# An encoder layer on one core: the first quarter of the MLP in a fixed block order, the residual's four VectorE transposes moved into the first block

## The chip, the core and the metric

The kernel runs on one core of a Trainium2 chip. A core has a matrix engine (TensorE, PE in the profile, with PEld for the loading of its stationary operand), a vector engine (VectorE, DVE), an activation engine (ScalarE, ACT), a general engine (GpSimd, POOL) and SyncE (SP), which here issues almost all transfers between the chip's memory and the core's buffers. Each engine works through its own list of instructions in order; the lists meet only in semaphores. The metric is the device time of one execution in microseconds (us), as the median of several runs.

## The reference

One layer of a streaming encoder for 256 tokens of width 2048, all in float32: a mixer (retention and a gated delta rule side by side), cross-attention into 256 memory tokens, and an MLP with squared ReLU, each with a norm ahead of it and a residual behind it. The change touches the passage from cross-attention into the MLP:

```python
    x = x + cross_attention(h, mem_n, w_xq[l], w_xkv[l], w_xo[l])
    h = rms_norm(x, norm_ffn_g[l])
    x = x + jnp.square(jax.nn.relu(h @ w_ff1[l])) @ w_ff2[l]
return rms_norm(x, norm_final_g)
```

`w_ff1` is 2048 x 8192, `w_ff2` 8192 x 2048.

## The kernel before

**Products.** Every float32 matrix is split into a rounded part and its remainder (`hi` and `lo`, both float32r), and a product is the sum of three partial products. Weights come in pieces of 1 MB: `fetch` (line 104) issues one transfer into a `raw` buffer of 128 x 2048, and for each half of it one ScalarE instruction that rounds (L125, `whi` from `raw`) and one VectorE instruction that subtracts (L126, `wlo` from `raw` and `whi`), each over 128 x 1024. There are three `raw` buffers and three of `whi` and of `wlo`. From the MLP on there is a fourth pair, `whx` and `wlx`, which `half_tiles` (line 79) hands out for every fourth half. Its pool (`mlp`, line 1117) takes the memory that the cross-attention's pool held until then.

**Blocks.** `blocks_in_steps` (line 192) computes 256 output columns for all tokens: two pieces of weights, so four halves, and for each half one *step* of 16 matmuls (L210; 8 of 128 x 512 on `whi`, 8 of 128 x 256 on `wlo`), spread over two accumulators `s0` and `s1`. Behind the last step each accumulator is read out (L219 on ScalarE, L220 on VectorE) and handed to an `evac` function. In the MLP that is `evac_h`: squared ReLU, and the split of the result into `hid`. The function takes a list `ends`. If it isn't empty, each matmul is issued after the last one that stands in it, and each step adds its last matmul to it: the steps are then held in the order of the code.

**What sets the order.** The kernel is written against a scheduler that orders each engine's list when the program is built, by priorities and by its own estimate of when things are ready. `tc.high_priority` lets a fetch overtake; `tc.issue_after(x)` puts an instruction behind `x`. What the scheduler chose is fixed in the program.

**The MLP.** It runs in four quarters of 2048 hidden columns (`fb`, line 1374): eight blocks with `w_ff1`, then products with `w_ff2`. Quarters 1 to 3 pass `ends` to their blocks; the first quarter passes `None`, so its steps may be interleaved. Below, A is the first block of the first quarter and B the second, with steps A0 to A3 and B0 to B3. The halves of A3 and B3 are `whx` and `wlx`.

**The residual.** `rt` holds the residual with features on the partitions. The output is wanted with tokens on the partitions, in `res`. Ahead of the first quarter four VectorE instructions (lines 1121 and 1122, STREAM_TRANSPOSE of 128 x 1024) transpose 32 x 32 squares of `rt` into `tr`, and `place` (line 1124), called behind each of the eight blocks, issues four transfers of 64 KB that put the squares in their places (L1129, `res` from `tr`, in runs of 128 bytes). A `place` needs all four transposes. `rt` and `tr` are later used as weight buffers.

**The norm.** Behind the last block of cross-attention's output projection, two small matmuls (L1042) add up the squares `acc2`; then come L1044 on VectorE, a power on POOL (L266) and L1113 on VectorE. Only the additions into `res`, much later, need their result.

Of the kernel before, what the change touches and what calls it, by code (L numbers as in the profile page):

```python
# [18 lines left out]
D = 2048  # L19
# [33 lines left out]
def trunk(ctx: ExitStack, tc: tile.TileContext, x_f, mem_f, positions, lead_f, small_f, w_in, ret_gn_g, w_out, w_xq,  # L53
# [3 lines left out]
    act, vec, pool, pe = nc.scalar, nc.vector, nc.gpsimd, nc.tensor  # L57
# [9 lines left out]
    def stream_ps():  # L67
        s0 = psp.tile([P, 512], F32, name="s0", tag="s0", bufs=2)
        s1 = psp.tile([P, 512], F32, name="s1", tag="s1", bufs=2)
        return s0, s1  # L70

    def bank():
        return psp.tile([P, 512], F32, name="b", tag="b", bufs=4)


    fetched, steps, latest = [], [], {}
# [18 lines left out]
    def step():  # L95
        if steps and next(steps[0], steps) is steps:
            steps.pop(0)
# [6 lines left out]
    def fetch(pieces, k, n, cuts=1, hold=None, at=(0, 0)):  # L104

        raw = wp.tile([P, k * n], F32, name="raw", tag="raw", bufs=3)
        rv = raw.rearrange("p (k n) -> p k n", k=k)
        with tc.high_priority(offset=100000):
            for off, ap in pieces:
                src = ap.rearrange("(k p) n -> p k n", p=P)  # L110
                for c in range(cuts):
                    ks = slice(c * k // cuts, (c + 1) * k // cuts)
                    fetched.append(nc.sync.dma_start(rv[:, ks, off:off + ap.shape[1]], src[:, ks, :]).ins)
            got = []
            for i in range(2):
                if hold:
                    both = hold().both
                    hi, lo = (both[:, a:a + 2, :].rearrange("p a s -> p (a s)") for a in (0, 2))
                else:
                    hi, lo = (h[:, a:a + k * n // 2] for h, a in zip(half_tiles(), at))  # L120
                src = raw[:, i * k * n // 2:(i + 1) * k * n // 2]
                part = k * n // max(cuts, 2)
                for c in range(0, k * n // 2, part):
                    cs = slice(c, c + part)
                    latest["hi"] = act.activation(hi[:, cs], src[:, cs], AF.Copy).ins  # L125
                    latest["lo"] = vec.tensor_sub(lo[:, cs], src[:, cs], hi[:, cs].bitcast(F32)).ins  # L126
                got.append((hi.rearrange("p (k n) -> p k n", n=n), lo.rearrange("p (k n) -> p k n", n=n)))
            latest["raw"] = fetched[-1]
        return got
# [20 lines left out]
    def quad_a():  # L150
        return new_quad(hqp, 5)
# [40 lines left out]
    def blocks_in_steps(quads, w, c0, nb, evac, ends=None, even=False):  # L192

        k = 16 // nb
        ps = stream_ps()
        n = nb * P
        for g in range(KT // k):  # L200
            halves = fetch([(0, w[g * k * P:(g + 1) * k * P, c0:c0 + n])], k, n, at=AT_BLOCKS)
            for h in range(2):
                these = [(i, b, part) for i in range(k // 2) for b in range(nb) for part in range(2)]
                if even and g == h == 0:
                    these.sort(key=lambda a: a[2])
                for i, b, part in these:
                    kk = (2 * g + h) * k // 2 + i
                    x = quads[kk // 4][0] if part else quads[kk // 4].both
                    with tc.issue_after(ends[-1]) if ends else ExitStack():
                        ins = pe.matmul(ps[b][:, :S] if part else ps[b], halves[h][part][:, i, b * P:(b + 1) * P],  # L210
                                        x[:, kk % 4, :], start=kk == 0 and not part, stop=kk == KT - 1 and part == 1).ins
                if ends is not None:
                    ends.append(ins)
                step()
                yield
        for b in range(nb):
            with tc.high_priority(offset=50000):
                o = sm.tile([P, S], F32, name="bo", tag="bo", bufs=2)
                act.activation(o, ps[b][:, S:], AF.Copy)  # L219
                vec.tensor_add(o, o, ps[b][:, :S])  # L220
                evac(b, o)

    def blocks(*args, **more):
        for _ in blocks_in_steps(*args, **more):
            pass
# [26 lines left out]
    with tc.high_priority(offset=300000):  # L252
# [3 lines left out]
        early = bank()  # L256
# [738 lines left out]
    rt = tp.tile([P, KT, S], F32, name="rt", tag="rt", bufs=1)  # L995
# [115 lines left out]
    h3, rstd3 = residual_pass(att, w_xo[0], G_FFN, "n3", between=values)  # L1111
# [6 lines left out]
    res = fp.tile([P, NT, D], F32, name="res", tag="res", bufs=1)  # L1118

    tr = fp.tile([P, KT, S], F32, name="tr", tag="tr", bufs=1)  # L1120
    for c in range(4):
        vec.transpose(*(a[:, 4 * c:4 * c + 4, :].rearrange("p k s -> p (k s)") for a in (tr, rt)))

    def place(b8):

        with tc.issue_after(fetched[-1]):
            for a in range(4):
                to = res[b8 % 4 * 32:b8 % 4 * 32 + 32, b8 // 4, :].rearrange("i (k a f) -> i k a f", a=4, f=32)[:, :, a, :]
                nc.sync.dma_start(to, tr[32 * a:32 * a + 32, :, b8 * 32:b8 * 32 + 32])  # L1129
# [44 lines left out]
    def token_sums(i, hs):  # L1174

        sv = fp.tile([P, 4, P], F32, name="sv", tag="sv", bufs=1)
        (a11, a21), (a12, a22) = ((hs[:, b, 0:P], hs[:, b, P:S]) for b in range(2))
        vec.tensor_add(sv[:, 0], a21, a22)
        vec.tensor_sub(sv[:, 1], sv[:, 0], a11)
        vec.tensor_sub(sv[:, 2], a11, a21)  # L1180
        vec.tensor_sub(sv[:, 3], a12, sv[:, 1])
        split([a[:, i, :] for a in s_hl], sv.rearrange("p a s -> p (a s)"))
# [190 lines left out]
    ends = []  # L1373
    for fb in range(4):
        hid = []
        rows = w_ff2[0, fb * D:(fb + 1) * D, :]
        early = fb > 0
        parts_of = with_seven(hid, rows, fb == 3, early)
        ends.clear()
        for b2 in range(8):  # L1380
            hs = fp.tile([P, 2, S], F32, name="hs", tag="hs", bufs=2)
            if b2 % 2 == 0:
                hid.append(quad_a())

            def evac_h(b, ps):
                if early:
                    act.activation(ps, ps, AF.Relu)
                    act.activation(hs[:, b, :], ps, AF.Square)
                else:
                    vec.scalar_tensor_tensor(hs[:, b, :], ps, 0.0, ps, op0=ALU.max, op1=ALU.mult)  # L1390
                qh, ql = (a[:, b2 % 2 * 2 + b, :] for a in hid[-1])
                act.activation(qh, hs[:, b, :], AF.Copy)
                vec.tensor_sub(ql, hs[:, b, :], qh.bitcast(F32))
                if b2 < 4 and b:
                    token_sums(b2, hs)

            blocks(h3, w_ff1[0], fb * D + b2 * 256, 2, evac_h, ends if early else None)
            if early and b2 > 2:
                next(parts_of)
            if fb == 0:  # L1400
                place(b2)
        for _ in parts_of:
            pass
# [42 lines left out]
```

## Time and profile before

| | |
|---|---|
| median of 3 runs | 2045.87 us (2045.28 to 2046.57) |
| the profiled execution: its own time | 2046.63 us |
| the profiled execution: span from first to last instruction | 2045.0 us |
| granted TensorE clock, mean over the span | 0.999 |
| 1 MB pieces of `w_ff1` and `w_ff2` into `raw` | 100 |
| transposes L1122 | 1360.0 to 1364.6 us of the span |
| place transfers L1129 | 1364.7 to 1421.9 us of the span |

The profile's page gives for each engine its busy time and share of the span, a chain of waits that is followed back from the last instruction, and groups of instructions by source line. The trace behind it answers finer questions: the timeline (instructions in order of time, with what ended the idle time ahead of each in square brackets), sums by stretches of time, and totals of who waited for whom. A matmul's shown duration is a latency: in a dense stream the next one starts before it ends, so that paces are read from starts. Lines of a queue (SPq) show the issue of transfers, not the transfers.

### The profile page before, as it was taken

The numbers are of one execution on the slowest core, as the hardware profiler recorded it, in microseconds if no ns is written. First come the engines' busy times: TensorE is split into PE (matmuls) and PEld (weight loads), VectorE is DVE, ScalarE is ACT, GpSimd is POOL, SyncE is SP. The second block draws the span as 40 slices with busy tenths as digits, with TensorE's granted clock in tenths as the row PEclk, the third lists the DMA queues.
The fourth block names the chain that finished last, engine by engine and source line by source line (L and its number), as shares of the span: only waits on it lengthen the run. The fifth ranks groups of instructions, "written<-read, shape, count | busy, mean of one in ns | idle before, by whom it ended". The sixth has DMA issues, their size and how long they took to land.

```text
span 2045.0 us, 28450 instructions
## 1 busy us (share of the span) xinstructions
PE 2032.4 (99%) x10802; PEld 1752.2 (86%) x10802; DVE 1548.7 (76%) x2422; ACT 1184.9 (58%) x1941; POOL 38.6 (2%) x50
## 2 busy tenths in 40 slices
PE   9999999999999999999999999999999999999998
PEld 8888888988888888888888899888888888888886
DVE  5887788779667875788567666777867887888788
ACT  6665764575457554755446565555546656656655
POOL 0000000000000000000000000000000000000000
PEclk9999999999999999999999999999999999999999
DMA  9679556456555655555467655569657656655761
GB/s 330 208 256 305 187 186 198 150 183 206 180 166 184 199 189 165 189 181 187 158 212 243 191 185 164 170 179 259 216 168 233 219 164 213 201 204 166 240 232 62
DMA packets 329225, 405.24 MB, mean 198 GB/s; under 512 B 34928, under 2 KB 239360, under 8 KB 328960
## 3 DMA queue, kind: packets, MB, share of 16 engines
q1 hardware_dynamic: 328656, 402.74, 61.3%
q8 instruction: 84, 1.38, 0.3%
q10 hardware_dynamic: 432, 0.69, 0.1%
q14 instruction: 53, 0.43, 0.1%
HBM read 389.74 MB, written 11.55 MB: 196 GB/s over the span
## 4 chain that ended last, share of the span: by engine, by line
PE 95%; DVE 2%; DMA 2%; ACT 1%; issue 0%; SPq 0%; POOLq 0%; POOL 0%; ACTq 0%; DVEq 0%
PE s L210 50%; PE s L167 8%; PE s L168 8%; PE s L166 8%; PE s L1212 7%; PE b L1212 7%; DMA raw<-w_ff 1%; PE s L400 1%; PE s L401 1%; PE s L402 1%; PE b L795 1%; PE b L698 1%; PE b L828 1%; PE b L138 0%; PE b L137 0%; PE b L139 0%
## 5 line engine op out<-in xcount | busy, mean ns | idle before, releaser
L210 PE MATMUL s<-q,whi 128*128 128x512 f32 x2816 | 968.7, 391 | 0.8 <-DVE bo L220 0.6
L126 DVE TENSOR_TENSOR wlo<-raw,whi 128x1024 fp32r<-128x1024 f32 x584 | 712.4, 1221 | 295.5 <-ACT whi L125 290.7
L125 ACT ACTIVATE whi<-raw 128x1024 fp32r<-128x1024 f32 x584 | 618.6, 1060 | 491.3 <-PE s L210 207.0
L210 PE MATMUL s<-q,wlo 128*128 128x256 f32 x2816 | 764.5, 281 | 0.4 <-DVE wlo L126 0.4
L210 PEld LDWEIGHTS s<-q,whi 128*128 128x128 f32 x2816 | 520.5, 188 | 101.7 <-DVE bo L220 0.9
L210 PEld LDWEIGHTS s<-q,wlo 128*128 128x128 f32 x2816 | 527.1, 188 | 13.2 <-DVE wlo L126 1.1
L167 PE MATMUL s<-wlo,q 128*128 128x512 f32 x704 | 277.3, 394 | 0.4 <-DVE wlo L126 0.4
L168 PE MATMUL s<-whi,q 128*128 128x512 f32 x704 | 274.9, 391 | 0.0
L166 PE MATMUL s<-whi,q 128*128 128x512 f32 x704 | 254.4, 391 | 0.0
L166 PEld LDWEIGHTS s<-whi,q 128*128 128x128 f32 x704 | 132.0, 188 | 27.3
L167 PEld LDWEIGHTS s<-wlo,q 128*128 128x128 f32 x704 | 132.3, 188 | 26.9 <-DVE wlo L126 0.8
L168 PEld LDWEIGHTS s<-whi,q 128*128 128x128 f32 x704 | 132.3, 188 | 26.3
L219 ACT ACTIVATE bo<-s 128x256 f32<-128x256 f32 x192 | 73.0, 380 | 108.5 <-PE s L210 108.4
L220 DVE TENSOR_TENSOR bo<-bo,s 128x256 f32<-128x256 f32 x192 | 79.7, 415 | 46.6 <-ACT bo L219 46.3
L1234 DVE TENSOR_TENSOR wlo<-rt,whi 128x1024 fp32r<-128x1024 f32 x56 | 68.1, 1223 | 32.8 <-ACT whi L1233 32.1
L125 ACT ACTIVATE whx<-raw 128x1024 fp32r<-128x1024 f32 x60 | 63.6, 1060 | 46.5 <-PE s L1212 19.1
L210 PE MATMUL s<-q,whx 128*128 128x512 f32 x256 | 89.2, 389 | 0.0
L1212 PE MATMUL s<-whi,q 128*128 128x512 f32 (+1 forms) x280 | 88.8, 383 | 0.0
L126 DVE TENSOR_TENSOR wlx<-raw,whx 128x1024 fp32r<-128x1024 f32 x60 | 73.3, 1221 | 19.2 <-ACT whx L125 18.8
L1233 ACT ACTIVATE whi<-rt 128x1024 fp32r<-128x1024 f32 x56 | 59.3, 1060 | 39.6 <-PE s L1212 20.2
L1212 PE MATMUL b<-whi,q 128*128 128x512 f32 x220 | 71.5, 389 | 0.0
L210 PE MATMUL s<-q,wlx 128*128 128x256 f32 x256 | 70.4, 280 | 0.0
(344 smaller groups left out, 2373.0 us busy)
## 6 DMA issues: line engine op xcount, KB each, us to landing
raw<-w_in SPq DMA_DIRECT2D x143, 1024.0 KB
raw<-w_ff SPq DMA_DIRECT2D x100, 1024.0 KB
raw<-w_xkv SPq DMA_DIRECT2D x29, 1024.0 KB
raw<-w_out SPq DMA_DIRECT2D x16, 1024.0 KB
raw<-w_xq SPq DMA_DIRECT2D x16, 1024.0 KB
raw<-w_xo SPq DMA_DIRECT2D x16, 1024.0 KB
rt<-w_ff SPq DMA_DIRECT2D x14, 1024.0 KB
tr<-w_ff SPq DMA_DIRECT2D x14, 1024.0 KB
```

What stands on the lines that cost most here:

```text
L125: latest["hi"] = act.activation(hi[:, cs], src[:, cs], AF.Copy).ins
L126: latest["lo"] = vec.tensor_sub(lo[:, cs], src[:, cs], hi[:, cs].bitcast(F32)).ins
L166: pe.matmul(o, xh, wh, start=first, stop=False)
L167: pe.matmul(o, xh, wl, start=False, stop=False)
L168: pe.matmul(o, xl, wh, start=False, stop=last)
L210: ins = pe.matmul(ps[b][:, :S] if part else ps[b], halves[h][part][:, i, b * P:(b + 1) * P], x[:, kk % 4, :], start=kk == 0 and not part, ...
L219: act.activation(o, ps[b][:, S:], AF.Copy)
L220: vec.tensor_add(o, o, ps[b][:, :S])
L400: pe.matmul(o, xh, wh, start=kk == 0 and c0 == 0, stop=False)
L1212: ins = pe.matmul(o, lhs[l], rhs[r], start=key not in opened, stop=last and j == 2, skip_group_check=True).ins
L1233: latest["hi"] = act.activation(hi, raw[:, c:c + 1024], AF.Copy).ins
L1234: latest["lo"] = vec.tensor_sub(lo, raw[:, c:c + 1024], hi.bitcast(F32)).ins
```

## The change

The four transposes are taken out of the place ahead of the MLP. The first block of the first quarter is run step by step, and behind each of its four steps one transpose is emitted, to be issued after the latest weight subtraction (`latest["lo"]`) at that point. All blocks of the first quarter now pass `ends`, so that each step's matmuls are issued after the previous step's last one. The number of instructions stays as it is.

```diff
-    for c in range(4):
-        vec.transpose(*(a[:, 4 * c:4 * c + 4, :].rearrange("p k s -> p (k s)") for a in (tr, rt)))
+    def transpose(c):
+        with tc.issue_after(latest["lo"]):
+            vec.transpose(*(a[:, 4 * c:4 * c + 4, :].rearrange("p k s -> p (k s)") for a in (tr, rt)))
...
-            blocks(h3, w_ff1[0], fb * D + b2 * 256, 2, evac_h, ends if early else None)
+            for n, _ in enumerate(blocks_in_steps(h3, w_ff1[0], fb * D + b2 * 256, 2, evac_h, ends)):
+                if fb == b2 == 0:
+                    transpose(n)
```

What the scheduler makes of it, at three places. Ahead of them, and on TensorE from the fourth block on, each engine's order is as it was; lines from 1122 on have one number more in the changed kernel.

TensorE behind step A2 (the first row is its last matmul). `s0_13017` and `s1_13018` are A's accumulators and `s0_13127`, `s1_13128` B's; `whi_13131` is the half of B0. Before:

```order
L210 MATMUL s1_13018<-q_12575,wlo_13064 128x256
L210 MATMUL s0_13127<-q_12127,whi_13131 128x512
L210 MATMUL s0_13127<-q_12127,wlo_13132 128x256
L210 MATMUL s1_13128<-q_12127,whi_13131 128x512
L210 MATMUL s1_13128<-q_12127,wlo_13132 128x256
L210 MATMUL s0_13127<-q_12127,whi_13131 128x512
L210 MATMUL s0_13127<-q_12127,wlo_13132 128x256
L1042 MATMUL b_12993<-ones_75,acc2_12125 128x2 x2
L210 MATMUL s1_13128<-q_12127,whi_13131 128x512
```

Now (`s0_13013` and `s1_13014` are A's accumulators, `whx_13065` and `wlx_13066` the halves of A3):

```order
L210 MATMUL s1_13014<-q_12575,wlo_13062 128x256
L1042 MATMUL b_12993<-ones_75,acc2_12125 128x2 x2
L210 MATMUL s0_13013<-q_12784,whx_13065 128x512
L210 MATMUL s1_13014<-q_12784,whx_13065 128x512
L210 MATMUL s0_13013<-q_12784,wlx_13066 128x256
L210 MATMUL s1_13014<-q_12784,wlx_13066 128x256
L210 MATMUL s0_13013<-q_12784,whx_13065 128x512
L210 MATMUL s0_13013<-q_12784,wlx_13066 128x256
```

Before, B0, B1, the first two matmuls of A3, the last of B1 and B2 stood ahead of the other 14 of A3; now all of A3 stands directly behind A2 and the norm's two matmuls, and B0 behind A3.

VectorE at the transposes. `wlo_13174` is the lower half of B2, `wlx_13068` (before) and `wlx_13066` (now) that of A3. Before:

```order
L126 TENSOR_TENSOR wlo_13136<-raw_13129,whi_13135 128x1024
L126 TENSOR_TENSOR wlo_13174<-raw_13171,whi_13173 128x1024
L1044 TENSOR_SCALAR n3_s_12996<-b_12993 128x2
L1122 STREAM_TRANSPOSE tr_13007<-rt_10152 128x1024 x4
L126 TENSOR_TENSOR wlx_13068<-raw_13061,whx_13067 128x1024
L1113 TENSOR_TENSOR rstd3q_13000<-n3_r_12998 128x2
```

Now:

```order
L126 TENSOR_TENSOR wlo_13136<-raw_13129,whi_13135 128x1024
L1044 TENSOR_SCALAR n3_s_12996<-b_12993 128x2
L1123 STREAM_TRANSPOSE tr_13007<-rt_10152 128x1024 x2
L126 TENSOR_TENSOR wlo_13174<-raw_13171,whi_13173 128x1024
L1113 TENSOR_TENSOR rstd3q_13000<-n3_r_12998 128x2
L126 TENSOR_TENSOR wlx_13066<-raw_13059,whx_13065 128x1024
L1123 STREAM_TRANSPOSE tr_13007<-rt_10152 128x1024 x2
```

The four transposes have become two and two, with the lower halves of B2 and A3 between them. ScalarE's order is unchanged here: the rounding for B2 (`whi_13173`) stands ahead of the one for A3 (`whx`).

SyncE's queue from the sixth `w_ff1` piece on (`raw_13282` is the second piece of the third block, `raw_13350` and `raw_13392` those of the fourth, `raw_13461` and `raw_13503` those of the fifth). Before:

```order
L113 DMA raw_13240<-w_ff1 128x8x256
L1129 DMA res_13006<-tr_13007 32x16x32 x2
L113 DMA raw_13282<-w_ff1 128x8x256
L1129 DMA res_13006<-tr_13007 32x16x32 x3
L113 DMA raw_13350<-w_ff1 128x8x256
L1129 DMA res_13006<-tr_13007 32x16x32 x4
L113 DMA raw_13392<-w_ff1 128x8x256
L1129 DMA res_13006<-tr_13007 32x16x32 x7
L113 DMA raw_13461<-w_ff1 128x8x256
```

Now:

```order
L113 DMA raw_13240<-w_ff1 128x8x256
L113 DMA raw_13282<-w_ff1 128x8x256
L1130 DMA res_13006<-tr_13007 32x16x32 x8
L113 DMA raw_13350<-w_ff1 128x8x256
L1130 DMA res_13006<-tr_13007 32x16x32 x4
L113 DMA raw_13392<-w_ff1 128x8x256
L1130 DMA res_13006<-tr_13007 32x16x32 x4
L113 DMA raw_13461<-w_ff1 128x8x256
```

One piece has moved ahead of all place transfers, and eight of these stand together behind it; by `raw_13461` both orders have issued the same pieces and the same sixteen place transfers.

## The prediction, made before the changed kernel was run

> **What bounds the kernel now.** I read the page's busy times and its chain of waits first, then sums by stages around the change, then the timelines of the engines that meet there.
>
> ```profile
> PE 2032.4 (99%) x10802; PEld 1752.2 (86%) x10802; DVE 1548.7 (76%) x2422; ACT 1184.9 (58%) x1941; POOL 38.6 (2%) x50
> PE 95%; DVE 2%; DMA 2%; ACT 1%; issue 0%; SPq 0%; POOLq 0%; POOL 0%; ACTq 0%; DVEq 0%
> ```
>
> TensorE is busy for 2032.4 of 2045.0 us: the kernel ends when its matmuls are through. Only 12.6 us are left, and the stage table (length, then busy us of PE, PEld, DVE, ACT, POOL, granted clock, share of the DMA engines, GB/s) shows how few of them lie near the change:
>
> ```profile
> 1340.00:1357.60 17.60, 17.60 (x105) 15.58 (x104) 13.18 (x21) 9.55 (x16) 0.00 (x0) 1.00 0.56 172
> 1357.60:1370.40 12.80, 12.22 (x73) 10.54 (x72) 10.12 (x12) 5.49 (x7) 0.69 (x1) 1.00 0.57 140
> 1370.40:1390.00 19.60, 19.60 (x116) 17.32 (x115) 15.05 (x30) 10.16 (x18) 0.00 (x0) 1.00 0.96 197
> 1390.00:1396.00 6.00, 5.60 (x33) 4.74 (x32) 3.15 (x8) 2.32 (x3) 0.00 (x0) 1.00 1.09 315
> 1396.00:1440.00 44.00, 44.00 (x256) 38.79 (x255) 32.81 (x51) 23.82 (x36) 0.00 (x0) 1.00 1.05 296
> ```
>
> TensorE idles 0.58 us in the second stretch and 0.40 us in the fourth, nowhere else in 100 us. The timeline has both (start, duration, what, idle ahead of it):
>
> ```profile
> 1369.07 0.28 PE L210 MATMUL s<-q,wlx 128*128 128x256 f32 x1
> 1369.94 0.50 PE L210 MATMUL s<-q,whi 128*128 128x512 f32 x1 [0.58 <-DVE bo L220]
> ...
> 1394.89 0.39 PE L210 MATMUL s<-q,whi 128*128 128x512 f32 x1
> 1395.68 0.39 PE L210 MATMUL s<-q,wlo 128*128 128x256 f32 x1 [0.40 <-DVE wlo L126]
> ```
>
> By starts they cost more, since a matmul's tail otherwise lies under the next one. In the dense stream below a `whi` matmul takes 0.23 us to the next start and a `wlo` one 0.115 (1357.60 to 1357.94 for the pair). The first hole is 0.87 - 0.115 = 0.75, the second 0.79 - 0.23 = 0.56; the first matmul behind each has 0.11 more than its pace. Together 0.86 + 0.67 = 1.53 us: all that the change can win here.
>
> **The change, part by part.** The first row below is the first matmul behind A2; the next four stand around the norm's matmuls:
>
> ```profile
> 1357.60 0.39 PE L210 MATMUL s<-q,whi 128*128 128x512 f32 x1
> ...
> 1357.94 0.39 PE L210 MATMUL s<-q,whi 128*128 128x512 f32 x1
> ...
> 1358.51 0.28 PE L210 MATMUL s<-q,wlo 128*128 128x256 f32 x1
> 1358.63 0.50 PE L1042 MATMUL b<-ones,acc 128*128 128x2 f32 x4
> 1358.99 0.47 PE L210 MATMUL s<-q,whi 128*128 128x512 f32 x1
> ```
>
> Six matmuls of B0 stand ahead of L1042 (the order's rows), 3 pairs of 0.34, so A2 ends its stream at 1357.60. Everything ahead of that keeps its order, so I keep that time. Now the other two engines:
>
> ```profile
> 1354.83 0.42 DVE L1028 TENSOR_TENSOR acc<-acc,sq 128x256 f32<-128x256 f32 x1
> 1356.34 1.23 DVE L126 TENSOR_TENSOR wlo<-raw,whi 128x1024 fp32r<-128x1024 f32 x1 [1.09 <-ACT whi L125]
> 1358.82 1.23 DVE L126 TENSOR_TENSOR wlo<-raw,whi 128x1024 fp32r<-128x1024 f32 x1 [1.25 <-ACT whi L125]
> 1359.96 0.15 DVE L1044 TENSOR_SCALAR n_s<-b 128x2 f32<-128x2 f32 x1
> 1360.03 4.61 DVE L1122 STREAM_TRANSPOSE tr<-rt 128x1024 f32<-128x1024 f32 x4
> 1364.56 1.18 DVE L126 TENSOR_TENSOR wlx<-raw,whx 128x1024 fp32r<-128x1024 f32 x1
> 1365.67 0.15 DVE L1113 TENSOR_TENSOR rstd3q<-n_r 128x2 f32<-128x2 f32 x1
> 1365.74 1.22 DVE L126 TENSOR_TENSOR wlo<-raw,whi 128x1024 fp32r<-128x1024 f32 x1
> ...
> 1357.72 1.06 ACT L125 ACTIVATE whi<-raw 128x1024 fp32r<-128x1024 f32 x1 [1.42 <-PE s L210]
> 1359.17 1.06 ACT L125 ACTIVATE whx<-raw 128x1024 fp32r<-128x1024 f32 x1 [0.38 <-PE b L1042]
> 1363.86 2.01 ACT L125 ACTIVATE whi<-raw 128x1024 fp32r<-128x1024 f32 x2 [3.63 <-DMA raw<-w_ff]
> ```
>
> Before, the halves of A3 were late (`wlx` done only at 1365.74, behind all four transposes), but TensorE did not wait: B0, B1 and B2, 8.3 us of matmuls, stood ahead. **The order that is now held takes this cover away.** Step by step:
> - L1042 runs from 1357.60, as `acc` is ready since 1355.25, and gives its result 0.50 later, at 1358.10. The next matmul could start 0.36 behind its start (1358.63 to 1358.99), at 1357.96.
> - ScalarE still rounds B2's half first (from 1357.72, released by A2's last read), then `whx`, which waits for L1042 as before. Two in a row take 2.01: done at 1359.73. The two `whx` matmuls can start 0.05 later, 1359.78, and are out at 1360.35 (2 x 0.23 + 0.11).
> - VectorE: L1044 at 1358.14 and transposes from 1358.21. Four took 1360.03 to 1364.56, 1.13 each, so two end their turn at 1360.48. Then `wlo` for B2, 1.12 to the next start (as 1364.56 to 1365.67): 1361.60; L1113, 0.07 (POOL's power, 0.69 us by the stage table, is through by then); `wlx` from 1361.67, 1.18: 1362.85.
> - TensorE takes up the other 14 matmuls of A3 0.05 later, at 1362.90 (as in the second hole, where the subtraction of the row below ends at 1395.63 and the matmul starts at 1395.68). They take 2.29 + 0.11: A3 ends at 1365.30. Without waits it would end at 1357.96 + 8 x 0.344 = 1360.71.
>
> ```profile
> 1394.40 1.23 DVE L126 TENSOR_TENSOR wlo<-raw,whi 128x1024 fp32r<-128x1024 f32 x1 [2.85 <-ACT whi L125]
> ```
>
> The new stall is **4.59 us**. Were two transposes, two subtractions and both small operations not pipelined, it would be 0.41 longer (1.20 + 1.20 + 1.23 + 1.18 + 0.30 against 4.71, with L1122's single duration taken as a quarter of 4.61 + 3 x 0.07): 5.0. Were `whx` alone the limit, with `wlx` right behind it at 1360.9, it would be 2.6.
>
> **What is given back.** The first hole waited for A's read-out, as A was finished only shortly ahead of the third block. Now A ends a whole block earlier, at 1365.30, and the third block starts at about 1376.3: that wait goes, 0.86. The second hole waited for the fifth block's first piece:
>
> ```profile
> 1366.20 6.75 DMA raw<-w_ff
> 1376.75 8.03 DMA raw<-w_ff
> 1386.69 6.51 DMA raw<-w_ff
> 1393.31 1.06 ACT L125 ACTIVATE whi<-raw 128x1024 fp32r<-128x1024 f32 x1 [4.05 <-DMA raw<-w_ff]
> ...
> 1364.72 1.39 SPq L1129 DMA_DIRECT2D res<-tr  x2
> 1378.08 8.51 SPq L1129 DMA_DIRECT2D res<-tr  x7
> ```
>
> In the chain a piece takes 6.5 to 8.0 us from issue to landing. Every transfer behind the transposes is the question here, and SP's queue is where it is decided: `raw_13282` now waits for `wlx`'s read of its buffer (1362.85), then eight place transfers for the last transpose (1365.2, before 1364.7), and `raw_13350`, `raw_13392`, `raw_13461` stand behind those. Seven of them took 8.51 when the engines were full. Eight then end at about 1373 to 1375, `raw_13350` lands by 1383 and is needed at 1387.3 - 2.4 (one rounding, one subtraction). By `raw_13461` the queue has issued what it had before, from a start 0.5 later with one piece already out: it should be issued at 1386 to 1388 and land by 1394.5. TensorE wants it at 1394.89 - 0.86 + 4.59 = 1398.6, less 2.4. So the second hole closes too, 0.67, with 1.7 us to spare.
>
> **Sum**: + 4.59 - 0.86 - 0.67 = **+3.1 us**. No instruction is added, and behind the fifth block TensorE alone sets the pace to the end, so the shift stays. The span goes from 2045.0 to 2048.1, the profiled execution's own time from 2046.63 to 2049.7; that one lay 0.76 above the median of the runs, 2045.87. I predict **2048.9**.
>
> About 0.2%, 4.1 us, is what a measurement of this kernel can tell from no change. The forecast is a loss below that.
>
> **Rivals.**
> - *The clock falls in the stall* (slower). TensorE would run 2 matmuls in the 4.9 us between 1358.0 and 1362.9. That idling costs the clock shows at the end of the span, behind the last matmul:
>
> ```profile
> 2035.68 0.28 PE L1212 MATMUL s<-whi,q 128*128 128x256 f32 x1
> ...
> 2036.00:2041.00 5.00, 0.00 (x0) 0.00 (x0) 3.35 (x12) 4.21 (x8) 0.84 (x2) 1.00 0.63 234
> 2041.20:2045.00 3.80, 0.00 (x0) 0.00 (x0) 0.00 (x0) 0.00 (x0) 0.00 (x0) 0.50 0.61 224
> ```
>
>  Full clock held for 5.0 us of idling, half of it was granted 0.2 us later. My longest gap is 2.55 us, half of that, which speaks against it; for it, that two matmuls may not count as work. If the clock fell all the same and took as long to return as there to fall (an estimate; no row shows a return), 5.2 us at half pace cost 2.6: 3.1 + 2.6, 2051.5. It decides from the idle length at which the clock gives way, anywhere between the 0.58 us that left it at 1.00 and 5 us. Chance 0.12. [...]
> - *The eight place transfers hold up the weights* (slower). If they take 1.75 each (as slow as 6.98 for four, in the row below), `raw_13461` slips by some 4 us to 1398.5 and TensorE waits 2 us: 2051. For it: the DMA share of 0.96 to 1.09 there. Against: the sixteen transfers ahead of that piece are the same as before. Chance 0.12.
>
> ```profile
> 1387.93 6.98 SPq L1129 DMA_DIRECT2D res<-tr  x4
> ```
>
> - *The change doesn't stall TensorE as I think* (not slower): `wlx` comes with `whx`, if the transposes take next to nothing where ScalarE is the later one. 2.6 - 1.5 = 1.1: 2047.0. Against it stands VectorE's list, in order. Chance 0.07.
>
> **How the numbers follow.** The forecast has 0.69; its own range, from a stall of 4.2 to 5.0 with 0.86 to 1.53 given back and half a microsecond of the median's own scatter, is 2048.1 to 2050.1. The 80% range, 2047.3 to 2051.0, takes in most of the rivals. Slower by over 0.2% (above 2049.96): both slower rivals and a little of the forecast's upper end, 0.28. Faster by over 0.2% would need 4.1 us where 1.53 lie idle: 0.02. Within: 0.70.
>
> **What would show it.** In the changed profile: VectorE with two transposes, a subtraction and then `wlx`; TensorE idle behind L1042 in two pieces, about 1.7 and 2.5 us, the second ended by `wlx`; no idle at the third and the fifth block. A granted clock under 1.00 in the 10 us behind would show the first rival, an idle ended by a `whi` or `wlo` of the fourth or fifth block behind a late DMA the second. I am wrong if TensorE doesn't wait at A3.

## The result, and the profile after

| | before | after |
|---|---|---|
| median | 2045.99 us (2044.80 to 2046.90, 8 runs) | 2051.32 us (2050.21 to 2052.48, 8 runs) |
| the profiled execution: its own time, span | 2046.63, 2045.0 | 2051.23, 2049.6 |
| granted clock, mean over the span | 0.999 | 0.997 |

The change makes the kernel slower: ratio 1.0027, 95% interval 1.0017 to 1.0038. That is 5.3 us where 3.1 were forecast, and 0.3 us above the upper end of the range. It is the case of the first rival.

The page after: busy times, and the chain of waits by engine.

```profile
PE 2034.2 (99%) x10802; PEld 1754.7 (86%) x10802; DVE 1551.3 (76%) x2422; ACT 1185.3 (58%) x1941; POOL 38.6 (2%) x50
PE 96%; DVE 2%; DMA 0%; issue 0%; ACT 0%; SPq 0%; POOLq 0%; POOL 0%; DVEq 0%; ACTq 0%
```

The same 10802 matmuls keep TensorE busy 1.8 us longer. No work was added, so some of it ran more slowly. TensorE's waits between 1350 and 1450 us (waiting line, what it waits for, total us, times, longest) are only two:

```profile
PE s L210 <- DVE wlx L126: 2.2, 1, 2.2
PE s L210 <- ACT whx L125: 1.7, 1, 1.7
```

Both old holes, in front of the third and the fifth block, are gone. The timeline of TensorE shows the new ones and what follows:

```profile
1357.73 0.50 PE L1042 MATMUL b<-ones,acc 128*128 128x2 f32 x4
1359.91 0.93 PE L210 MATMUL s<-q,whx 128*128 128x512 f32 x2 [1.68 <-ACT whx L125]
1363.07 0.80 PE L210 MATMUL s<-q,wlx 128*128 128x256 f32 x2 [2.23 <-DVE wlx L126]
1363.67 0.63 PE L210 MATMUL s<-q,whx 128*128 128x512 f32 x1
...
1364.31 0.63 PE L210 MATMUL s<-q,whx 128*128 128x512 f32 x1
...
1366.87 0.51 PE L210 MATMUL s<-q,whx 128*128 128x512 f32 x1
...
1367.33 0.39 PE L210 MATMUL s<-q,whi 128*128 128x512 f32 x1
```

Up to 1363.07 this is the predicted stall: idle in two pieces, the second ended by `wlx`. Behind it a pair of matmuls takes 0.64 us (1363.67 to 1364.31) where the dense stream before took 0.344, until about 1367. The other two engines did what the prediction said, in the same order and nearly at the same times:

```profile
1358.35 2.36 DVE L1123 STREAM_TRANSPOSE tr<-rt 128x1024 f32<-128x1024 f32 x2
1360.63 1.18 DVE L126 TENSOR_TENSOR wlo<-raw,whi 128x1024 fp32r<-128x1024 f32 x1
1361.73 0.15 DVE L1113 TENSOR_TENSOR rstd3q<-n_r 128x2 f32<-128x2 f32 x1
1361.80 1.22 DVE L126 TENSOR_TENSOR wlx<-raw,whx 128x1024 fp32r<-128x1024 f32 x1
1362.93 2.37 DVE L1123 STREAM_TRANSPOSE tr<-rt 128x1024 f32<-128x1024 f32 x2
...
1358.82 1.04 ACT L125 ACTIVATE whx<-raw 128x1024 fp32r<-128x1024 f32 x1
```

The cause of the slow matmuls stands in the table by stretches (length, busy us of PE, PEld, DVE, ACT, POOL with their instructions, granted clock, share of the DMA engines, GB/s). It is cut at 1360.28 and 1367.10, where the clock changes, and every 3.41 us between and around them. That is half of the 6.83 us at half clock here, and all of the time at half clock in the runs with the transposes behind B and with A free (below). Two expectations call such a stretch a window.

```profile
1356.86:1360.28 3.42, 1.74 (x12) 1.46 (x11) 2.85 (x4) 2.00 (x2) 0.70 (x1) 1.00 0.34 82
1360.28:1363.69 3.41, 1.18 (x5) 0.62 (x4) 3.41 (x5) 0.00 (x0) 0.00 (x0) 0.50 0.69 225
1363.69:1367.10 3.41, 3.41 (x12) 2.93 (x12) 1.61 (x2) 0.00 (x0) 0.00 (x0) 0.50 0.74 212
1367.10:1370.52 3.42, 3.42 (x21) 3.03 (x21) 2.93 (x7) 1.94 (x4) 0.00 (x0) 1.00 0.93 187
```

The clock is halved at 1360.28, in the middle of the stall, and comes back at 1367.10. Only the first gap, 1.68 us, lies ahead of the fall; the second begins at 1360.84 (1359.91 + 0.93), when the clock is at half already. The matmuls recorded in a stretch of 3.41 us are 21 at full clock and 12 at half.

**Where the time went.** Without a wait, A3 would have ended 0.36 + 8 x 0.344 behind the start of L1042 at 1357.73: 1360.84. B0 starts at 1367.33, 6.49 us late. At full clock the 14 matmuls behind the first `wlx` pair's start would have ended 2.40 after 1363.07, at 1365.47. So the late data cost 4.63 and the clock 1.86. Less the two holes, 1.53, that is +4.96; the medians differ by 5.3 (3.5 to 7.8 by the interval), the two spans by 4.6.

### The profile page after: what moved, and what is told of

Read it like the earlier page. It is cut to its first block, busy times and chain, and to the rows that moved or that the text cites. A ratio compares the mean times of both kernels' runs of the same rounds, so it can differ in the third digit from the quotient of the medians.

```text
span 2049.6 us, 28451 instructions
## 1 busy us (share of the span) xinstructions
PE 2034.2 (99%) x10802; PEld 1754.7 (86%) x10802; DVE 1551.3 (76%) x2422; ACT 1185.3 (58%) x1941; POOL 38.6 (2%) x50
## 4 chain that ended last, share of the span: by engine, by line
PE 96%; DVE 2%; DMA 0%; issue 0%; ACT 0%; SPq 0%; POOLq 0%; POOL 0%; DVEq 0%; ACTq 0%
PE s L210 51%; PE s L167 8%; PE s L168 8%; PE s L166 8%; PE s L1213 7%; PE b L1213 7%; PE s L400 1%; PE s L401 1%; PE s L402 1%; PE b L795 1%; PE b L828 1%; PE b L138 0%; PE b L137 0%; PE b L698 0%; PE b L139 0%
## 5 line engine op out<-in xcount | busy, mean ns | idle before, releaser
L219 ACT ACTIVATE bo<-s 128x256 f32<-128x256 f32 x192 | 73.0, 380 | 118.7 <-PE s L210 118.6
```

## The experiments

The theory now: the held order leaves TensorE nothing to do until `whx` and `wlx` come (about 3.1 us net), and this idling halves the clock (about 1.9 more). Rivals: the held order or the divided transposes cost something of their own; the slow pace belongs to the place transfers, not to the clock. Each run below has the kernel before beside it on the same chip. An edit is shown against the changed kernel where nothing else is said.

**The order alone.** The transposes stay ahead of the MLP (the edit is against the kernel before).

```diff
-            blocks(h3, w_ff1[0], fb * D + b2 * 256, 2, evac_h, ends if early else None)
+            blocks(h3, w_ff1[0], fb * D + b2 * 256, 2, evac_h, ends)
```

> The order held in all quarters, the four transposes left ahead of the MLP. By the theory (A3 held ahead of B loses its cover, and VectorE reaches A3's lower half only behind the transposes): four transposes instead of two stand ahead of it, so TensorE waits about 2.3 us longer than in the changed kernel (second gap 4.5 instead of 2.2 us), the clock falls as well, and the time is 2 to 4 us above the changed kernel's: 7 to 9 us over before. By the rival that the place of the transposes is what costs, and the order is harmless: as before, within 1 us.

Measured: 2053.72 us (5 runs; before 2046.09), ratio 1.0039, interval 1.0027 to 1.0052. TensorE's waits and the stretches at half clock:

```profile
PE s L210 <- DVE wlx L126: 4.4, 1, 4.4
...
1359.35:1362.76 3.41, 0.81 (x2) 0.09 (x1) 3.41 (x4) 0.00 (x0) 0.00 (x0) 0.50 0.72 229
1362.76:1366.18 3.42, 1.65 (x5) 1.47 (x6) 1.72 (x3) 0.00 (x0) 0.00 (x0) 0.50 0.57 73
1366.18:1369.59 3.41, 3.41 (x12) 2.92 (x11) 0.57 (x2) 0.99 (x2) 0.00 (x0) 0.50 0.82 191
```

With all four transposes ahead of `wlx` its wait is 4.4 instead of 2.2 us, and half clock lasts three stretches. The loss is in the order; dividing the transposes makes it smaller.

**The transposes alone.** As the change, but the first quarter's blocks stay free.

```diff
-            for n, _ in enumerate(blocks_in_steps(h3, w_ff1[0], fb * D + b2 * 256, 2, evac_h, ends)):
+            for n, _ in enumerate(blocks_in_steps(h3, w_ff1[0], fb * D + b2 * 256, 2, evac_h, ends if early else None)):
```

> The transposes moved into the first block's steps, the first quarter's order left free. By the theory: B0 to B2 stand ahead of the rest of A3 again, no wait behind step A2, clock at 1.00 all through the MLP, time within 1.5 us of before (-1.5 to +1). By the rival that the moved transposes and the place transfers behind them are what costs: 3 to 5 us over before.

Measured: 2048.60 us (2047.02 to 2049.81, 11 runs; before 2046.09), ratio 1.0011, 1.0002 to 1.0020. Slower by 2.5, which I had not expected. No wait behind A2, but one elsewhere (TensorE, then ScalarE):

```profile
1371.23 0.73 PE L210 MATMUL s<-q,whx 128*128 128x512 f32 x2 [2.80 <-ACT whx L125]
...
1368.90 1.06 ACT L125 ACTIVATE whi<-raw 128x1024 fp32r<-128x1024 f32 x1 [3.75 <-DMA raw<-w_ff]
1369.86 0.36 ACT L219 ACTIVATE bo<-s 128x256 f32<-128x256 f32 x1
1370.13 1.05 ACT L125 ACTIVATE whx<-raw 128x1024 fp32r<-128x1024 f32 x1
```

The scheduler has put the rounding of a half of the third block ahead of A's read-out (L219) and of `whx` for B3. ScalarE waits 3.75 us for that piece's transfer, and B3, whose data were there, waits behind it. TensorE waits nowhere for a transpose here; their new place changed what the scheduler chose on another engine. In this profile, of the fastest of the 11 runs, the clock stayed at 1.00. Whether it fell in others isn't shown; their spread of 2.8 us is hardly wider than that of the kernel before beside them (2044.88 to 2047.62).

**A free, the other blocks held.** Is it the later blocks' freedom or the order around A and B that costs this?

```diff
-            for n, _ in enumerate(blocks_in_steps(h3, w_ff1[0], fb * D + b2 * 256, 2, evac_h, ends)):
+            for n, _ in enumerate(blocks_in_steps(h3, w_ff1[0], fb * D + b2 * 256, 2, evac_h, ends if early or b2 else None)):
```

> The changed kernel, but block A alone isn't held in order; the blocks behind it are. By the view that the order around A3 and B3 decides, this kernel has the order of the run with the transposes alone (B0 and more behind A2, ScalarE's rounding for the third block ahead of whx for B3), so it should give that run's time, 2048 to 2049.5: no wait behind A2, a gap of 2.5 to 3.3 us at B3 that a whx ends, clock 1.00. If that run lost its 2.5 us because the later blocks were free, this one gives 2045 to 2046.5.

Measured: 2050.55 us (2049.51 to 2052.25, 9 runs; before 2046.76), ratio 1.0021, 1.0011 to 1.0030. The gap of 2.8 us at B3 is there again, and a second one of 0.8 in front of `wlx`. The time is a good 1 us above what I expected. In this profile the clock was halved, for one stretch, which I had not counted on:

```profile
1368.83:1372.24 3.41, 1.57 (x10) 1.12 (x8) 0.55 (x2) 1.33 (x3) 0.00 (x0) 1.00 1.08 195
1372.24:1375.66 3.42, 1.65 (x7) 1.14 (x8) 3.42 (x7) 1.49 (x3) 0.00 (x0) 1.00 0.98 276
1375.66:1379.07 3.41, 3.41 (x12) 2.91 (x11) 2.68 (x10) 2.04 (x5) 0.00 (x0) 0.50 1.12 161
```

So the freedom of the later blocks isn't what cost those 2.5 us: with it gone, the wait at B3 is as long.

**Filling the stall.** The changed kernel with 18 more matmuls between A2 and A3. They read operands that are ready and write a bank that nothing reads.

```diff
+                    if n == 2:
+                        spot = bank()
+                        for _ in range(18):
+                            with tc.issue_after(ends[-1]):
+                                ends.append(pe.matmul(spot, h3[0][0][:, 0, 0:P], h3[0].both[:, 0, :], start=True, stop=True).ins)
```

> The changed kernel with 18 matmuls of 128 x 512 more, into an accumulator that nobody reads, between A2 and A3, where TensorE waits. By the theory (the clock falls because TensorE idles there, and comes back only two windows later): the halves of A3 come at the same time as in the changed kernel, but the clock stays at 1.00 and A3 runs at full pace, so the time is about 1.9 us under the changed kernel's: 3 to 3.5 us over before. By the rival that A3 is slow for another reason (transposes or transfers beside it): A3's 14 matmuls take 4.3 us as in the changed kernel, and the time stays at 5 over before or more.

Measured: 2049.52 us (2048.16 to 2050.57, 11 runs; before 2046.09), ratio 1.0015, 1.0006 to 1.0024: +3.4. The steps' order and the transposes are those of the change. So are the transfers, but for one piece of weights that is issued behind four place transfers instead of eight; TensorE waits for weights in neither. Work without any use, put into the idle time, makes the kernel faster by almost 2 us (2049.52 against 2051.32, with the kernel before at 2046.09 and 2045.99 beside them). The stall's stretch:

```profile
1357.60:1365.30 7.70, 7.56 (x38) 6.12 (x37) 7.19 (x9) 2.21 (x4) 0.51 (x1) 1.00 0.74 203
```

What is left of the loss is the late data, which the filling doesn't bring earlier. The slow pace was the clock's.

**Filling with 7, and with 12.** How much idling does the clock bear? 7 cover the first gap alone, 12 also shorten the second (in the change they are 1.68 and 2.23 us, 3.91 together; the edits are against the run with 18).

```diff
-                        for _ in range(18):
+                        for _ in range(7):
```

```diff
-                        for _ in range(18):
+                        for _ in range(12):
```

> The run with matmuls that fill the stall, with 7 in the place of 18: they cover the first gap of 1.7 us alone, the second of 2.2 us in front of wlx stays. If the clock goes by the longest gap or by both gaps as one idle stretch of over 3 us, it holds at 1.00 here and the time is that of the stall without the clock: 2049 to 2049.6. If 2.2 us of idling are enough for it, one window of half clock or more follows, 1.7 us more: 2050.5 to 2051.5.

> The run with 7 filling matmuls, with 12: five more at 0.23 each shorten the gap in front of wlx from 2.4 to about 1.25 us, and A3 ends no earlier. If a gap of about 1.7 us or more within one stretch of 3.4 us is what halves the clock (the run with 7 fell with 1.75 us of idling in such a stretch, the run with the transposes alone held with 1.23 and 1.57 in two neighbouring ones), the clock holds in every execution: no time under 1.00 in the MLP, and the time is that of the data wait alone, 4.6 - 1.5, 2048.5 to 2050, as with 18. If any gap of over about 1 us can halve it, 2050.5 to 2052 as with 7.

Measured: with 7, 2051.99 us (2049.09 to 2052.70, 11 runs; before 2046.76), ratio 1.0024, 1.0015 to 1.0034; with 12, 2049.90 (2048.31 to 2051.04, 11 runs; before 2046.35), ratio 1.0017, 1.0008 to 1.0026. Two rows of TensorE's timeline of each, first with 7, then with 12: the first `wlx` pair and the start of B0.

```profile
1363.28 0.80 PE L210 MATMUL s<-q,wlx 128*128 128x256 f32 x2 [2.42 <-DVE wlx L126]
...
1367.72 0.63 PE L210 MATMUL s<-q,whi 128*128 128x512 f32 x1
```

```profile
1363.36 0.50 PE L210 MATMUL s<-q,wlx 128*128 128x256 f32 x2 [1.49 <-DVE wlx L126]
...
1365.77 0.39 PE L210 MATMUL s<-q,whi 128*128 128x512 f32 x1
```

`wlx` comes within 0.1 us of the same time. With 7, B0 starts 4.44 us later, with 12 only 2.41. In these profiles one gap of 2.42 us, with dense work ahead of it, halved the clock (1.75 of it lay ahead of the fall, 3.41 - 1.66 in the first row below); one of 1.49 didn't. The stretches at the changes of the clock with 7 show how it came back:

```profile
1359.21:1362.62 3.41, 1.66 (x7) 0.73 (x5) 3.41 (x5) 0.87 (x1) 0.20 (x1) 1.00 0.94 268
1362.62:1366.03 3.41, 2.75 (x9) 2.46 (x10) 2.89 (x3) 0.00 (x0) 0.00 (x0) 0.50 0.47 126
1366.03:1369.45 3.42, 3.42 (x12) 2.84 (x12) 1.46 (x3) 2.02 (x4) 0.00 (x0) 0.50 1.12 271
```

**The change once more.** Does the clock's fall stand at a fixed distance behind the last dense matmul?

> The changed kernel once more, one profile, on the same chip as the run beside it. The waits should be the same, 1.7 us for whx and 2.2 us for wlx. If the clock goes by busy time in stretches of 3.4 us that run on from the start of the program, and not by the distance from the matmuls, the fall comes at another distance behind the norm's matmuls than the 2.55 us of the first profile, and lasts one, two or three such stretches (3.4, 6.8 or 10.2 us).

Measured, one run: 2049.96 us, before 2045.60. The same two waits (1.7, 2.4) and again 6.83 us at half:

```profile
1356.22 0.50 PE L1042 MATMUL b<-ones,acc 128*128 128x2 f32 x4
...
1356.06:1359.47 3.41, 1.39 (x8) 0.83 (x7) 2.84 (x5) 2.00 (x2) 0.70 (x1) 1.00 0.51 128
1359.47:1362.89 3.42, 1.33 (x5) 1.23 (x6) 3.42 (x5) 0.00 (x0) 0.00 (x0) 0.50 0.57 193
1362.89:1366.30 3.41, 3.41 (x12) 2.92 (x12) 1.19 (x2) 0.67 (x2) 0.00 (x0) 0.50 0.94 264
```

The fall comes 3.25 us behind the start of L1042; in the first profile it was 2.55. So the moment of the fall doesn't hang on the last matmuls alone.

**The transposes behind block B.** Held order, but `wlx` with no transpose ahead of it.

```diff
-                if fb == b2 == 0:
-                    transpose(n)
+                if fb == 0 and b2 == 1 and n == 3:
+                    for c in range(4):
+                        transpose(c)
...
-            if fb == 0:
-                place(b2)
+            if fb == 0 and b2:
+                place(b2 - 1)
+                if b2 == 7:
+                    place(7)
```

> The order held as in the changed kernel, all four transposes moved on behind the second block's last step, each block's place calls one block later. By the theory: A3 still waits for ScalarE, which rounds B2's half and then A3's (first gap 1.7 us as in the changed kernel), and VectorE has only one subtraction ahead of A3's, so the second gap shrinks from 2.2 to about 0.7 us: a wait of 2.6 to 2.9 us in all, less the 1.5 us of holes that go: 1 to 1.5 us over before if the clock stays, 2 to 3 if it falls as in the changed kernel. By the rival that the transposes don't matter: 5 us over before.

Measured: 2050.41 us (2047.10 to 2051.64, 11 runs; before 2046.09), ratio 1.0019, 1.0010 to 1.0028: +4.3, where I expected 2 to 3 with a fall of the clock and 5 if the transposes didn't matter. The interval, 2.0 to 5.7 us, holds all of these, so that the time doesn't decide between them. The waits do: that for `wlx` shrank from 2.2 to 0.5 us, and the clock was at half for one stretch. Part of the surplus was in view: from 1390 to 1440 us TensorE got through 285 matmuls, where the change had 292 at the same clock of 1.00 (by starts, a pair of them took 0.353 us instead of 0.345). I ran it again to see whether that goes with the kernel.

> The kernel with the transposes behind block B once more, one profile: in its first profile TensorE ran some 2% slower between 1365 and 1440 us (285 matmuls recorded from 1390 to 1440 where the changed kernel had 292), at a clock of 1.00, about 1.9 us in all, which its waits don't explain. If that goes with the kernel (its transfers, its order), it is there again: 283 to 287 in that stretch and 2050 to 2051.5. If it goes with the execution, 290 to 293 and 2048 to 2049.3.

Measured, one run: 2049.71 us, before 2045.60. First the first profile's row, then the second's:

```profile
1390.00:1440.00 50.00, 50.00 (x285) 43.35 (x284) 34.75 (x56) 24.85 (x38) 0.00 (x0) 1.00 0.99 254
```

```profile
1390.00:1440.00 50.00, 50.00 (x293) 44.33 (x292) 35.31 (x57) 25.18 (x37) 0.00 (x0) 1.00 0.97 248
```

The slower pace isn't the kernel's: it is gone, and yet the run is 4.1 above the one beside it. By the second profile (waits of 1.7 and 0.8 us, then A3's 14 matmuls, all but the last three at half clock) B0 started 4.6 late; less 1.53 that is 3.1. The other 1 us I have not located; two single runs can differ by that much through scatter alone (the 21 runs of the kernel before beside the one with 12 filling matmuls lie between 2044.78 and 2048.98), so it isn't shown that there is a loss to be found.

**The fourth pair of buffers from B on.** The changed kernel, but A3 gets an ordinary pair, whose rounding doesn't wait for the norm's matmuls; `whx` and `wlx` are first used at B3.

```diff
-    spare.append(fp)
...
+                    if n == 3:
+                        spare.append(fp)
```

> The changed kernel, order held, but the fourth pair of half buffers is handed out only behind block A, so that A3 uses an ordinary pair whose rounding doesn't wait for the norm's matmuls. If the loss is the late whx and wlx at A3 and the clock that falls there, TensorE has no wait behind A2, the clock stays at 1.00, the two old holes (0.86 and 0.67) are gone or one of them is, and the time is between 1.5 under and 0.5 above the kernel before: 2044.6 to 2046.6. If the held order or the divided transposes cost something of their own further on (weights late at B2 or B3 by 0.5 to 2 us), 2047 to 2048.5.

Measured: 2045.64 us (2045.04 to 2047.10, 11 runs; before 2046.76), ratio 0.9997, 0.9988 to 1.0006. TensorE's only wait between 1320 and 1560 us stands in this stretch, at B2, where `wlo` is 0.24 us late:

```profile
1366.00:1367.20 1.20, 0.96 (x6) 0.53 (x5) 1.20 (x3) 1.04 (x1) 0.00 (x0) 1.00 0.74 96
```

The order is held as in the change, and nothing of the 5.3 us is left: by the interval, holding it costs 1.2 us at most. The division of the transposes is not tested here. They are emitted one by one, but the scheduler put all four together, as before:

```profile
1359.63 4.62 DVE L1123 STREAM_TRANSPOSE tr<-rt 128x1024 f32<-128x1024 f32 x4
```

They end long before B3 wants its `wlx`. It is also the version with the lowest median: 1.1 us under the kernel before beside it, too little to be told from no change.

**Both.** This, with the transposes divided among the steps of B in the place of A (the edit is against the run before this one).

```diff
-                if fb == b2 == 0:
-                    transpose(n)
-                    if n == 3:
-                        spare.append(fp)
+                if fb == b2 == 0 and n == 3:
+                    spare.append(fp)
+                if fb == 0 and b2 == 1:
+                    transpose(n)
...
-            if fb == 0:
-                place(b2)
+            if fb == 0 and b2:
+                place(b2 - 1)
+                if b2 == 7:
+                    place(7)
```

> Fourth pair of buffers handed out behind block A, as in the run that did this alone, and the four transposes divided among the steps of block B in the place of A (their place transfers one block later). If nothing but the waits at A3 and B2 and the clock matter, TensorE has at most 0.5 us of waits between 1340 and 1450 us, the clock stays at 1.00, and the time is that run's within 0.5: 2045.2 to 2046.2, against the kernel before in the same call 0.3 to 1.3 faster, too little to be told from no change. If the later place transfers hold up weights, a wait of 0.5 us or more behind a late DMA at the fourth to sixth block and 2046.5 to 2048.

Measured: 2046.16 us (2044.96 to 2049.62, 11 runs; before 2046.35), ratio 1.0000, 0.9991 to 1.0009. The same single wait of 0.2 us, clock 1.00. Here VectorE does divide the transposes:

```profile
1359.50 2.36 DVE L1123 STREAM_TRANSPOSE tr<-rt 128x1024 f32<-128x1024 f32 x2
1361.78 1.18 DVE L126 TENSOR_TENSOR wlx<-raw,whx 128x1024 fp32r<-128x1024 f32 x1
1362.89 2.36 DVE L1123 STREAM_TRANSPOSE tr<-rt 128x1024 f32<-128x1024 f32 x2
```

With A3's data on time, four together or two and two make no difference that can be measured. They run at nearly the same time in both versions, so that these two say nothing on other places.

## Why the prediction was wrong

- **The stall's data: right.** 4.59 us forecast, 4.63 measured; `wlx` was forecast to end at 1362.85 and ended at 1363.02 (1361.80 + 1.22), with L1042 0.13 later than forecast. The gaps were forecast at about 1.7 and 2.5 and were 1.68 and 2.23.
- **What is given back: right.** Both holes closed, 1.53 us.
- **The place transfers: right.** They didn't hold up the weights. In SP's queue the eight took 0.78 each, where that rival needed 1.75, and the next piece was issued ahead of the forecast of about 1373 to 1375:

```profile
1365.37 6.25 SPq L1130 DMA_DIRECT2D res<-tr  x8
1371.72 0.56 SPq L113 DMA_DIRECT2D raw<-w_ff  x1
```

- **The clock: wrong.** The step that failed is "Full clock held for 5.0 us of idling, half of it was granted 0.2 us later. My longest gap is 2.55 us, half of that, which speaks against it", and with it the chance of 0.12 for that rival. I read one duration from the end of the span and took it as a limit for a gap. That end, cut every 3.41 us ahead of and behind the fall at 2041.14, says something else:

```profile
2034.31:2037.72 3.41, 1.65 (x14) 1.45 (x13) 3.38 (x10) 2.03 (x5) 0.55 (x1) 1.00 0.00 0
2037.72:2041.14 3.42, 0.00 (x0) 0.00 (x0) 1.67 (x6) 2.49 (x4) 0.56 (x1) 1.00 0.97 358
2041.14:2044.55 3.41, 0.00 (x0) 0.00 (x0) 0.00 (x0) 0.00 (x0) 0.00 (x0) 0.50 0.70 256
```

 Behind the first stretch, with 1.65 us busy, the clock held; behind the second, with none, it fell. Of the 5.2 us until the fall, 1.8 lay in a stretch behind which it held. In the changed kernel the first gap, 1.68 us, lay whole in one stretch of 3.41 us (1356.86 to 1360.28) with 1.74 busy, and the clock fell; the longer gap came behind the fall. So my reading now, an estimate from these stretches and those of the experiments, is that the fall goes by how much work one stretch holds, not by the length of a gap.
- **The rival's price** (2.6 us, for a return as long as the fall) was too high by 0.7: the clock was at half for 6.83 us, but in the first 3.41 TensorE was busy for only 1.18 and otherwise waited. Its time, 2051.5, was nearly met by luck, because the median took 0.4 us more than the +4.96 of the sum; that the clock falls in the stall was right. The 80% range was said to take in most of the rivals, but it ended at 2051.0, below this one. (By its own terms the forecast's range should also have reached 2050.5, not 2050.1: 5.0 less 0.86, and half a microsecond, on 2045.87. The measured time lies above both.)

## What to carry to other kernels

A free order that puts another block's matmuls ahead of a late operand is cover. Before holding an order, look for the operand that comes last in each step (here the pair of buffers whose first rounding waits for a small matmul) and have that one come earlier, or use it later. Price an idle TensorE twice: the wait itself (4.63 us here) and the half clock that can come behind it (1.86 here, behind a stretch of 3.41 us with 1.68 idle). Don't go by the longest gap: with the transposes alone a gap of 2.80 us left the clock at 1.00, and in the change one of 1.68 was enough. What went with the fall in these runs was how little work lay in one such stretch.

## What the runs showed that I had not expected

- **Half clock came in whole stretches of 3.41 us** in the MLP: 3.41 us with the transposes behind B and with A free, 6.83 in both profiles of the change and with 7 filling matmuls, 10.24 with the order alone. The clock stayed at half behind stretches with up to 2.75 us busy (7 filling matmuls) and came back behind 2.94 (transposes behind B, first profile) and 3.41. The times at full clock are whole numbers of them too: in the first profile of the change 1351.68 us from the start of the clock's record at 8.60 to the fall, 396 of 3.413, and 675.84 us from the return to the fall at the end, 198; in the kernel before 2034.34 us, from 6.80 to 2041.14, 596.
- **In these runs the clock fell behind stretches with little work.** By shown busy time it fell behind 1.74 (change, and the transposes behind B), 1.73 (the order alone), 1.66 (7 fills), 1.65 (A free), 1.39 (change again) and 0.94 us (transposes behind B again), and held behind 1.57 (A free) and 1.65 (end of the kernel before). These figures overlap, as they count each matmul's tail and 0.50 us for the norm's matmuls of two columns. An estimate by pace separates them: with 0.23 us from its start for each 128x512 and 0.115 for each 128x256, the most work behind which the clock fell is 1.26 us, the least behind which it held 1.39, in two neighbouring stretches of the run with A free: about two fifths of 3.41. With 12 fills and with the transposes alone every stretch had more, and the clock held (the bounds of these stretches are an estimate, as the clock doesn't change there):

```profile
1359.62:1363.03 3.41, 2.25 (x10) 1.50 (x8) 3.41 (x5) 0.54 (x1) 0.00 (x0) 1.00 0.94 275
```

```profile
1366.24:1369.65 3.41, 2.18 (x13) 1.66 (x12) 0.92 (x1) 0.75 (x1) 0.00 (x0) 1.00 1.13 244
1369.65:1373.07 3.42, 1.84 (x9) 1.59 (x10) 3.08 (x5) 1.80 (x4) 0.00 (x0) 1.00 0.93 254
```

 Across the last two lay a gap of 2.80 us, longer than either of the change's; by the estimated bounds it is cut in two. If that is why the clock held, a stall's price depends on where it meets a bound. The bounds did move from one execution to the next: the fall came 2.55 us behind the start of L1042 in the first profile of the change and 3.25 in the second. That the bound's place decides is not shown by a run of its own.
- **A pace 2% slower at full clock** over at least 50 us of one execution (transposes behind B, 285 matmuls for 292), gone in the next of the same kernel. Its cause is open.
